# Two latent attentions: fp32 probabilities times values-and-ones in one plain product, in place of two-part products and a running sum

## The chip, the cores and the metric

The kernel runs on one core of a Trainium2 chip. The metric is the device time of one launch in microseconds (us), lower is better; a launch covers the whole network below. A core has five engines with instruction queues of their own: TensorE (PE; its weight loads are shown apart as PEld), VectorE (DVE), ScalarE (ACT), GpSimd (POOL) and SyncE (SP), which here issues every DMA.

## The reference

A two-layer network over 1024 latent tokens and 128 context tokens, 1024 channels, all in fp32. The mixers of the latent tokens are what matters here.

```python
# layer 0, multi-head latent attention: 8 heads, query/key width 96, value width 64, 1024 latent + 128 context keys
s = einsum('bqhd,bkhd->bhqk', q, k) * 96**-0.5
p = softmax(s, axis=-1)
out = einsum('bhqk,bkhd->bqhd', p, v)

# layer 1, neighbourhood attention: 16 heads of width 64, window of 8 x 16 grid positions, plus all 128 context keys
s_loc = einsum('bqhd,bikhd->bhqik', qr, kb) * 64**-0.5 + bias        # masked outside the window
s_ctx = einsum('bqhd,blhd->bhql', qr, k_ctx) * 64**-0.5
p = softmax(concat([s_loc, s_ctx]), axis=-1)
out = p_loc @ vb + p_ctx @ v_ctx
```

Around them: modulated norms, a combined input projection with a pooling mixer (layer 0), output projections, and a squared-relu MLP of width 4096 in each layer. The context tokens have small attentions of their own, which the change leaves as they are.

## The kernel before

**Number formats.** TensorE is fed in two ways. A tile of type F32R (shown as fp32r where DVE or ACT writes it) goes through as one product; where the accuracy of fp32 is wanted, an operand is split into two F32R tiles, high = rounded value, low = value minus high, and the products of the parts are added in PSUM (`mm3`). A product of two F32 tiles is a "plain" product.

**Stages.** Layer 0: input projection, norms, keys and queries; then the maxima of heads 0 and 1 woven with the values (`value_gen`), then the latent attention over heads 0 to 7 (`attend_units` woven with `max_units` of head h+2), then the output projection in two groups of tokens (`out_group`, helper `mm3`, lines L336 to L338, tile `ps_o`, residual at L891) while the rest of the modulation vectors is computed on DVE (`ada_gen`, L201, tile `trash`) and the attention's results are split (`split_groups`, L876 and L877, tile `oa`); then the MLP. Layer 1: projection, values (`value_gen1`), then the neighbourhood attention over heads 0 to 15 (`na_units` woven with `na_max` of head h+2, and for heads 0 to 6 with the context tokens' attention), then output projection and MLP. Loads of a head's operands are issued one or two heads ahead. What a scheduler makes of the program sets the order on each engine: it follows the written order of the units and may move independent instructions across each other.

**A unit of layer 0** is one head, 512 queries (a half), 128 keys. Scores come transposed, keys on partitions: three products into `ps_st` (L1079, L1082, L1083). ACT then takes the exponential twice from PSUM, once as F32R (`phi`, L1086) and once as F32 (`p`, L1087; for the first key tile straight into `ac`). DVE subtracts, `plo` = p - phi (L1088); POOL adds p to the running sum `ac` (L1090); and TensorE multiplies both parts with the values into `ps_pv` (L1091, L1092). 9 key tiles x 2 halves x 8 heads make 144 units. Each head's block of the stored values is 128 columns wide: 64 high parts and 64 low parts, so one product gives both; `split_values` (L998 on ACT, L999 on DVE) makes it, `vd0` and `vd` hold it in DRAM.

**The end of a half** (`finish_half`): ACT copies one half of the partitions of `ps_pv` (L1048), DVE adds it to the other (L1049); later, through the list `deferred`, a plain product of 64 columns of ones with `ac` (L1053, tile `ps_d`) sums the probabilities over the partitions, ACT copies that to `den` (L1054), and every second head `recip_pair` divides.

**A head of layer 1** takes the 128 context keys for each half (512 queries each; `ctx_unit`: exponentials into `chb` and `ac`, difference `clb`, L1326 to L1330, L1319) and 8 key tiles, of which two meet 256 queries and six 384, cut at the border of the halves (L1348 to L1357). Maxima (`na_max`) are 8 blocks of 512 columns, read by DVE (L1297).

**Buffers.** Large tiles share 36 slots, taken in the order in which they came free. A pair of units holds three slots before (`p`, `phi`, `plo`); `ac` takes a fourth in layer 0. PSUM tag "pa" (3 banks) serves `ps_st`, `ps_d`, `ps_o` and others, "pb" (3) the maxima, "pc" (2) `ps_pv`.

Of the kernel before, what the change touches and what calls it, by code (L numbers as in the profile page):

```python
# [10 lines left out]
F32 = mybir.dt.float32  # L11
# [79 lines left out]
def hybrid_kernel(ctx: ExitStack, tc: tile.TileContext, I, O):  # L91
# [255 lines left out]
    # Tokens go through in two groups of two halves of HC.  The first product takes hidden tiles j and j + NB, both  # L347
    # halves of the channels and both halves of the group as 2 x 2 blocks and forms the four results from seven products.
# [150 lines left out]
    # ================= layer 0 =================  # L499
# [29 lines left out]
    vd0 = DR("vd0", [9, P, D])  # L529

# [268 lines left out]
    vp = S.alloc("vp")  # L799

    def value_gen():
        for tt in range(10):
            ps = PS("ps_v")
            if tt < 9:
                ck = slice(tt * P, tt * P + P)
                nc.tensor.matmul(ps, ckv[0][:, ck], wk[1][:, 512:], start=True, stop=False)
                nc.tensor.matmul(ps, ckv[1][:, ck], wk[0][:, 512:], start=False, stop=False)
                nc.tensor.matmul(ps, ckv[0][:, ck], wk[0][:, 512:], start=False, stop=True)
            else:
                nc.tensor.matmul(ps, ckvc, wkf[:, 512:], start=True, stop=True)  # L810
            if tt == 8:
                nc.scalar.copy(vp[:, :512], ps)
            else:
                vs = S.alloc("vst", F32R)
                split_values(vs[:, :D], ps)
                dma(vd0[min(tt, 8)], vs[:, :D])
                S.free(vs)
            yield
        S.free(*ckv, small)
        S.free_ap(wkf)  # L820
# [160 lines left out]
    def load_rest(h):  # L981
        ql, kl, v = (S.alloc(n, F32R) for n in ("ql", "kl", "v"))
        n0, r0 = 64 * (h % 2), 32 * (h % 4)
        dma(ql[0:64, :NS], qd_n[1][h // 2, n0:n0 + 64, :])
        dma(ql[64:96, :NS], qd_r[1][h // 4, r0:r0 + 32, :])
        dma(kl[0:64, :], kd_n[1][h // 2, n0:n0 + 64, :])
        dma(kl[64:96, :], kd_r[1][h // 4, r0:r0 + 32, :])
        load_v(vd0, h, v)
        return ql, kl, v

    def load_v(vd, h, v):
        dma(v.rearrange("p (t f) -> p t f", t=9), vd[:, :, P * h:P * h + P].rearrange("t p f -> p t f"))
# [52 lines left out]
    def finish_half(par, half, po, ac, opair, den, last, store=None, ac_slot=True):  # L1045
        qs = slice(half * 512, half * 512 + 512)
        a = T("pva")
        nc.scalar.copy(a[par:par + 64], po[64 - par:128 - par])  # L1048
        nc.vector.tensor_add(opair[par:par + 64, qs], po[par:par + 64], a[par:par + 64])  # L1049

        def sums():
            pd = PS("ps_d")
            nc.tensor.matmul(pd[par:par + 64], ones[:, 0:64], ac[:, qs], start=True, stop=True)  # L1053
            nc.scalar.copy(den[par:par + 64, qs], pd[par:par + 64])  # L1054
            if half and ac_slot:
                S.free(ac)
            if last:
                recip_pair(opair, den)
                if store is not None:
                    dma(store, opair[:, :NS])  # L1060
                    S.free(opair)

        deferred.append(sums)

    def attend_units(h, qk, rest, opair, den):
        (qh, kh), (ql, kl, vv) = qk, rest
        v = vv.rearrange("p (t f) -> p t f", t=9)
        ac = S.alloc("ac")
        held = None
        for half in range(2):  # L1070
            qs = slice(half * 512, half * 512 + 512)
            po = PS("ps_pv", "pc")
            for kt in range(9):
                if held is None:
                    held, n = (S.alloc("p"), S.alloc("phi", F32R), S.alloc("plo", F32R)), 0
# [8 lines left out]
                p_ = ac[:, qs] if kt == 0 else held[0][:, u]  # L1084
                h_, l_ = held[1][:, u], held[2][:, u]
                nc.scalar.activation(h_, ps, AF.Exp, scale=scale0)  # L1086
                nc.scalar.activation(p_, ps, AF.Exp, scale=scale0)  # L1087
                nc.vector.tensor_sub(l_, p_, h_)  # L1088
                if kt:
                    nc.gpsimd.tensor_add(ac[:, qs], ac[:, qs], p_)  # L1090
                nc.tensor.matmul(po, v[:, kt, :], h_, start=kt == 0, stop=False)  # L1091
                nc.tensor.matmul(po, v[:, kt, :], l_, start=False, stop=kt == 8)  # L1092
                n += 1
                if n == 2:
                    S.free(*held)
                    held = None
# [3 lines left out]
            finish_half(64 * (h % 2), half, po, ac, opair, den, half and h % 2)  # L1100
# [46 lines left out]
    # ================= layer 1 =================  # L1147
# [29 lines left out]
    vd = DR("vd1", [9, P, 2 * D])  # L1177
# [21 lines left out]
    for i in range(2):  # L1199
        vs = S.alloc("vst", F32R)  # L1200
        split_values(vs[:, :D], vr[:, i * 512:i * 512 + 512])
        dma(vd[8][:, i * D:i * D + D], vs[:, :D])
        S.free(vs)
    S.free(vr)

# [62 lines left out]
    def load_na_rest(h):  # L1268
        k2, q2, v, tb = S.alloc("k2", F32R), W("wh", "q2"), S.alloc("nv", F32R), W("wr", "tb")
# [7 lines left out]
        load_v(vd, h, v)  # L1277
# [26 lines left out]
    def na_units(h, tl, rest, opair, den):  # L1304
# [3 lines left out]
        ac, chb, clb = W("wr", "ac"), W("wh", "chb"), W("wl", "clb")  # L1308
# [9 lines left out]
        def close_half(half):  # L1318
            nc.tensor.matmul(po[half], v3[:, 8, :], clb[:, half * 512:half * 512 + 512], start=False, stop=True)  # L1319
            finish_half(par, half, po[half], ac, opair, den, half and h % 2, od[h // 2][:, :NS] if h < 14 else None, False)  # L1320

        def ctx_unit(half):
# [3 lines left out]
            nc.scalar.activation(chb[:, qs], ps, AF.Exp)  # L1326
            nc.scalar.activation(ac[:, qs], ps, AF.Exp)
            nc.vector.tensor_sub(clb[:, qs], ac[:, qs], chb[:, qs])  # L1328
            po[half] = PS("ps_pv", "pc")
            nc.tensor.matmul(po[half], v3[:, 8, :], chb[:, qs], start=True, stop=False)  # L1330
# [4 lines left out]
        for i in range(8):  # L1335
# [3 lines left out]
            if held is None:  # L1339
                held, cnt = (S.alloc("p"), S.alloc("phi", F32R), S.alloc("plo", F32R)), 0  # L1340
            a, b = max(i - 1, 0) * P, min(i + 2, 8) * P
            n = b - a
            o = cnt * CH
            p_, hb, lb = (t[:, o:o + n] for t in held)
# [3 lines left out]
            nc.scalar.activation(hb, ps, AF.Exp)  # L1348
            nc.scalar.activation(p_, ps, AF.Exp)
            nc.vector.tensor_sub(lb, p_, hb)  # L1350
            nc.gpsimd.tensor_add(ac[:, a:b], ac[:, a:b], p_)  # L1351
            for half in range(2):
# [3 lines left out]
                for t in (hb, lb):  # L1356
                    nc.tensor.matmul(po[half][:, u - half * 512:w - half * 512], v3[:, i, :], t[:, u - a:w - a],  # L1357
                                     start=False, stop=False)
            cnt += 1
            if cnt == 3 or i == 7:  # L1360
                S.free(*held)
# [10 lines left out]
    def value_gen1():  # L1372
        for qt in range(4):
            ws = [wsplit(I["wv1"][qt, i]) for i in range(2)]
            fs = slice(qt * 256, qt * 256 + 256)
            for tt in range(9):
# [9 lines left out]
                else:  # L1386
                    if tt % 2 == 0:
                        vs = S.alloc("vst", F32R)
                    o = 512 * (tt % 2)
                    split_values(vs[:, o:o + 512], ps)  # L1390
                    if tt % 2:
                        dma(vd[tt - 1:tt + 1, :, qt * 512:qt * 512 + 512].rearrange("t p f -> p t f"),
                            vs[:, :D].rearrange("p (t f) -> p t f", t=2))
# [218 lines left out]
```

## Time and profile before

| | |
|---|---|
| timed runs | 3104.63 us median of 3 (3103.17 to 3110.44) |
| span of the profiled execution | 3107.1 us, mean granted TensorE clock 0.961 |
| its own time | the page gives the span alone; it lies between the timed runs |
| busy | PE 2968.8 us (96%), DVE 2427.3 (78%), ACT 1490.6 (48%), POOL 661.8 (21%) |
| layer 0 attention, first score product to last value product | 313.7 to 591.7 us |
| layer 0 output projection, up to the MLP's first product | 591.7 to 721.2 us |
| layer 1 attention, first context score product to last value product | 1890.1 to 2235 us |

Rows of groups read: line, engine, operation, names (out<-in), shapes, count | busy us, mean ns of one | idle time before them and what ended it. TensorE's records are pipelined: a product's recorded duration is longer than the distance to the next one's start. A plain product of the program stands as two records in the profile, so the 48 products of L1053 are 96 records. PEclk is the granted TensorE clock as a share of full speed. Window rows give, for each engine, its busy us and its instructions, then PEclk, the DMA engines' busy share and GB/s.

### The profile page before, as it was taken

The page shows a single profiled execution, that of the slowest core. Times are in us where ns is not written, and L with a number is a line of the kernel's source. Part 1 is how long each engine was busy: PE and PEld are TensorE (multiplying, and loading weights), DVE is VectorE, ACT ScalarE, POOL GpSimd, SP SyncE. Part 2 cuts the span into 40 slices and gives each one's busy share as a digit, 9 for nine tenths or more (in the row PEclk, how much of TensorE's full clock was granted, in tenths as well). Part 3 has the DMA queues.
Part 4 walks back from the last instruction along what each step waited for, and adds up shares of the span by engine and source line. Part 5 has one row for each costly group of instructions (what it writes and reads, how often), then busy time and mean ns, then how long its engine had stood idle before and what let it go on. Part 6 is the DMA issues. An engine that isn't in the chain of part 4 may idle for free.

```text
span 3107.1 us, 48559 instructions
## 1 busy us (share of the span) xinstructions
PE 2968.8 (96%) x18718; PEld 2673.4 (86%) x18718; DVE 2427.3 (78%) x4124; ACT 1490.6 (48%) x2546; POOL 661.8 (21%) x423
## 2 busy tenths in 40 slices
PE   7998998889999999999999999999999999999999
PEld 4956665689999999999988797666799999999999
DVE  5977999998668889786899534789777768877775
ACT  5364666434436534453645423667434445443433
POOL 1014777543000020000221002355421000010000
PEclk9996999899999999999999898899999999999999
DMA  6529222342223334232566345578302332332322
GB/s 229 165 71 319 63 60 48 121 136 84 90 85 92 103 129 143 89 96 87 169 206 199 108 178 151 151 186 227 127 28 76 95 95 79 114 93 87 102 75 85
DMA packets 148280, 376.03 MB, mean 121 GB/s; under 512 B 14225, under 2 KB 62977, under 8 KB 148050
## 3 DMA queue, kind: packets, MB, share of 16 engines
q1 hardware_dynamic: 148050, 372.94, 39.3%
q8 instruction: 147, 2.41, 0.3%
q14 instruction: 83, 0.68, 0.1%
HBM read 310.69 MB, written 61.01 MB: 120 GB/s over the span
## 4 chain that ended last, share of the span: by engine, by line
PE 67%; DVE 7%; DMA 3%; issue 2%; ACT 1%; POOL 1%; SPq 0%; DVEq 0%; POOLq 0%; ACTq 0%
PE ps L453 9%; PE ps L455 9%; PE ps L454 9%; PE ps L423 8%; PE ps L425 7%; PE ps L424 7%; PE ps_n L338 2%; PE ps_n L337 2%; PE ps_n L336 2%; PE ps_v L1381 1%; PE ps_v L1382 1%; PE ps_v L1383 1%; DVE trash L201 1%; DMA tb<-in_bias_k 1%; PE ps_o L336 1%
## 5 line engine op out<-in xcount | busy, mean ns | idle before, releaser
L453 PE MATMUL ps<-ml,wh 128*128 128x288 f32 x2048 | 591.9, 295 | 10.3 <-DVE ml L442 7.8
L454 PE MATMUL ps<-mh,wl 128*128 128x288 f32 x2048 | 600.8, 295 | 0.0
L455 PE MATMUL ps<-mh,wh 128*128 128x288 f32 x2048 | 596.5, 295 | 0.0
L423 PE MATMUL ps<-bl,wh 128*128 128x288 f32 x1792 | 532.7, 297 | 13.4 <-DVE bl L354 10.2
L424 PE MATMUL ps<-bh,wl 128*128 128x288 f32 x1792 | 529.5, 295 | 0.0
L425 PE MATMUL ps<-bh,wh 128*128 128x288 f32 x1792 | 527.9, 295 | 0.0
L453 PEld LDWEIGHTS ps<-ml,wh 128*128 128x128 f32 x2048 | 381.2, 188 | 11.3 <-DVE ml L442 8.3
L454 PEld LDWEIGHTS ps<-mh,wl 128*128 128x128 f32 x2048 | 385.2, 188 | 0.0
L455 PEld LDWEIGHTS ps<-mh,wh 128*128 128x128 f32 x2048 | 383.2, 188 | 0.1
L459 DVE SCALAR_TENSOR_TENSOR x<-ps,ada,x 128x288 f32<-128x288 f32 (+2 forms) x640 | 269.3, 450 | 113.2 <-PE ps L455 112.1
L423 PEld LDWEIGHTS ps<-bl,wh 128*128 128x128 f32 x1792 | 336.7, 188 | 16.7 <-issue 11.5
L425 PEld LDWEIGHTS ps<-bh,wh 128*128 128x128 f32 x1792 | 338.3, 189 | 0.0
L424 PEld LDWEIGHTS ps<-bh,wl 128*128 128x128 f32 x1792 | 337.3, 188 | 0.2
L396 ACT CAST wh<-s 128x512 fp32r<-128x512 f32 x256 | 146.1, 618 | 302.1 <-PE ps L455 216.1
L161 ACT CAST wh<-wr 128x1024 fp32r<-128x1024 f32 x188 | 196.9, 1049 | 177.3 <-PE ps L425 79.9
L162 POOL TENSOR_TENSOR wl<-wr,wh 128x1024 fp32r<-128x1024 f32 x44 | 119.6, 2723 | 731.4 <-ACT wh L161 722.8
L201 DVE CUSTOM_DVE_ANT_0 trash<-wada,silu 128x1024 bf16<-128x1024 f32 x160 | 216.1, 1351 | 17.9 <-DMA wada<-in_wada 6.2
L1351 POOL TENSOR_TENSOR ac<-ac,p 128x384 f32<-128x384 f32 (+1 forms) x128 | 151.8, 1186 | 367.2 <-DVE clb L1328 221.3
L1090 POOL TENSOR_TENSOR ac<-ac,p 128x512 f32<-128x512 f32 x128 | 202.9, 1587 | 67.1 <-ACT p L1087 35.0
L162 DVE TENSOR_TENSOR wl<-wr,wh 128x1024 fp32r<-128x1024 f32 x144 | 179.9, 1252 | 42.5 <-ACT wh L161 42.0
L396 ACT CAST wh<-wr 128x1024 fp32r<-128x1024 f32 (+1 forms) x128 | 106.9, 836 | 220.8 <-PE ps L455 150.7
L272 POOL TENSOR_TENSOR nt<-nt,sq 128x288 f32<-128x288 f32 (+1 forms) x45 | 50.7, 1129 | 706.8 <-ACT sq L271 697.5
(341 smaller groups left out, 7080.7 us busy)
## 6 DMA issues: line engine op xcount, KB each, us to landing
wr<-in_w SPq DMA_DIRECT2D x256, 512.0 KB
wada<-in_wada SPq DMA_DIRECT2D x48, 512.0 KB
wada<-in_wada0t SPq DMA_DIRECT2D x32, 512.0 KB
vd<-vst SPq DMA_DIRECT2D x27, 512.0 KB
wr<-in_win SPq DMA_DIRECT2D x24, 512.0 KB
wr<-in_wout SPq DMA_DIRECT2D x24, 512.0 KB
kk<-kd SPq DMA_DIRECT2D x32, 288.0 KB
nv<-vd SPq DMA_DIRECT2D x16, 576.0 KB
```

Of the source, the lines that this page charges most:

```text
L161: nc.scalar.copy(hi, r)
L162: (nc.gpsimd if e else nc.vector).tensor_sub(lo, r, hi)
L201: nc.vector.tensor_tensor_reduce(trash, r[:, :D], silu[i][:, :D], scale=1.0, scalar=0.0, op0=ALU.mult, op1=ALU.add, accum_out=a)
L396: nc.scalar.copy(h, src)
L423: nc.tensor.matmul(ps, wh[:, a], hl[:, b], start=k == 0, stop=False)
L424: nc.tensor.matmul(ps, wl[:, a], hh[:, b], start=False, stop=False)
L425: nc.tensor.matmul(ps, wh[:, a], hh[:, b], start=False, stop=k == 3)
L453: nc.tensor.matmul(ps, wh, hl, start=kk == 0, stop=False)
L454: nc.tensor.matmul(ps, wl, hh, start=False, stop=False)
L455: nc.tensor.matmul(ps, wh, hh, start=False, stop=kk == 3)
L459: nc.vector.scalar_tensor_tensor(x[m][:, a:b], ps[:, a - ch * HC:b - ch * HC], g, x[m][:, a:b], op0=ALU.mult, op1=ALU.add)
L1090: nc.gpsimd.tensor_add(ac[:, qs], ac[:, qs], p_)
```

## The change

Both attentions keep the probabilities whole, as F32, and the stored values as F32 in blocks of 192 columns for a pair of heads: values of the even head, 64 ones, values of the odd head. A head reads 128 of them (values and ones), so that one plain product per key tile gives the weighted values on 64 partitions and the sum of the probabilities on the other 64. Gone are the second exponential, the subtraction, POOL's running sum, the product with ones (L1053) and the addition at the end of a half; `finish_values` copies the values on DVE and the sums on ACT. `place_values` stores the values: a memset of ones on POOL and one copy on ACT.

```diff
     def load_rest(h):
-        ql, kl, v = (S.alloc(n, F32R) for n in ("ql", "kl", "v"))
+        ql, kl, v = S.alloc("ql", F32R), S.alloc("kl", F32R), S.alloc("v")
...
-    def split_values(o, src):
-        s4 = src.rearrange("p (g e f) -> p g e f", e=2, f=64)
-        o4 = o.rearrange("p (g e f) -> p g e f", e=4, f=64)
-        hi, lo = o4[:, :, 0:4:3], o4[:, :, 1:3]
-        nc.scalar.copy(hi, s4)
-        nc.vector.tensor_sub(lo, s4, hi)
+    def place_values(o, src):
+        o4 = o.rearrange("p (g e f) -> p g e f", e=3, f=64)
+        nc.gpsimd.memset(o4[:, :, 1], 1.0)
+        nc.scalar.copy(o4[:, :, 0:3:2], src.rearrange("p (g e f) -> p g e f", e=2, f=64))
+    def load_pv(vd, h, v):
+        o = 192 * (h // 2) + 64 * (h % 2)
+        dma(v.rearrange("p (t f) -> p t f", t=9), vd[:, :, o:o + P].rearrange("t p f -> p t f"))
+    def finish_values(par, half, po, opair, den, last, store=None):
+        qs = slice(half * 512, half * 512 + 512)
+        nc.vector.tensor_copy(opair[par:par + 64, qs], po[par:par + 64])
+        nc.scalar.copy(den[par:par + 64, qs], po[64 - par:128 - par])
+        def divide():
+            recip_pair(opair, den)
+            if store is not None:
+                dma(store, opair[:, :NS])
+                S.free(opair)
+        if last:
+            deferred.append(divide)
...
-    def finish_half(par, half, po, ac, opair, den, last, store=None, ac_slot=True):
...
     def attend_units(h, qk, rest, opair, den):
-        ac = S.alloc("ac")
-                    held, n = (S.alloc("p"), S.alloc("phi", F32R), S.alloc("plo", F32R)), 0
+                    held, n = S.alloc("p"), 0
-                p_ = ac[:, qs] if kt == 0 else held[0][:, u]
-                h_, l_ = held[1][:, u], held[2][:, u]
-                nc.scalar.activation(h_, ps, AF.Exp, scale=scale0)
+                p_ = held[:, u]
                 nc.scalar.activation(p_, ps, AF.Exp, scale=scale0)
-                nc.vector.tensor_sub(l_, p_, h_)
-                if kt:
-                    nc.gpsimd.tensor_add(ac[:, qs], ac[:, qs], p_)
-                nc.tensor.matmul(po, v[:, kt, :], h_, start=kt == 0, stop=False)
-                nc.tensor.matmul(po, v[:, kt, :], l_, start=False, stop=kt == 8)
+                nc.tensor.matmul(po, v[:, kt, :], p_, start=kt == 0, stop=kt == 8)
...
     def na_units(h, tl, rest, opair, den):
-        ac, chb, clb = W("wr", "ac"), W("wh", "chb"), W("wl", "clb")
+        cp = W("wr", "cp")
-            nc.scalar.activation(chb[:, qs], ps, AF.Exp)
-            nc.scalar.activation(ac[:, qs], ps, AF.Exp)
-            nc.vector.tensor_sub(clb[:, qs], ac[:, qs], chb[:, qs])
+            nc.scalar.activation(cp[:, qs], ps, AF.Exp)
-            nc.tensor.matmul(po[half], v3[:, 8, :], chb[:, qs], start=True, stop=False)
+            nc.tensor.matmul(po[half], v3[:, 8, :], cp[:, qs], start=True, stop=False)
-            nc.scalar.activation(hb, ps, AF.Exp)
             nc.scalar.activation(p_, ps, AF.Exp)
-            nc.vector.tensor_sub(lb, p_, hb)
-            nc.gpsimd.tensor_add(ac[:, a:b], ac[:, a:b], p_)
-                for t in (hb, lb):
-                    nc.tensor.matmul(po[half][:, u - half * 512:w - half * 512], v3[:, i, :], t[:, u - a:w - a],
-                                     start=False, stop=False)
+                nc.tensor.matmul(po[half][:, u - half * 512:w - half * 512], v3[:, i, :], p_[:, u - a:w - a],
+                                 start=False, stop=i == (4, 7)[half])
```

In layer 0's units TensorE's order before, for heads 0 to 5 (L1079, L1082, L1083 are the scores, L1091 and L1092 the value products, L1022 the maxima of a later head, L1053 the product with ones):

```order
L1079 MATMUL ps_st<-qh_2906,kl_3217 128x512
L1082 MATMUL ps_st<-ql_3216,kh_2907 128x512
L1083 MATMUL ps_st<-qh_2906,kh_2907 128x512
L1092 MATMUL ps_pv<-plo_3591,v_3218 128x512
L1091 MATMUL ps_pv<-phi_3590,v_3218 128x512
L1022 MATMUL ps_m<-kh_3546,qh_3545 128x384
L1053 MATMUL ps_d<-ac_3235,ones 64x512
L1092 MATMUL ps_pv<-plo_3591,v_3218 128x512
L1091 MATMUL ps_pv<-phi_3622,v_3218 128x512
```

And now at such a place (scores L1072, L1075, L1076, values L1079, maxima L1036):

```order
L1036 MATMUL ps_m<-kh_3258,qh_3257 128x384
L1072 MATMUL ps_st<-qh_2812,kl_3026 128x512
L1075 MATMUL ps_st<-ql_3025,kh_2813 128x512
L1076 MATMUL ps_st<-qh_2812,kh_2813 128x512
L1079 MATMUL ps_pv<-p_3313,v_3027 128x512
L1036 MATMUL ps_m<-kh_3258,qh_3257 128x384
```

Each unit has one value product where it had two, and it stands behind the scores of a later unit.

DVE's order before, at the last half of head 7 (L1088 is the subtraction, L1049 the addition, L876 and L877 the split for the output projection):

```order
L1049 TENSOR_TENSOR o_722_4491<-ps_pv,pva 64x512
L876 CAST oa_4973<-pooled_928 128x576
L1088 TENSOR_TENSOR plo_4875<-p_4873,phi_4874 128x512
L877 TENSOR_TENSOR oa_4973<-pooled_928,oa_4973 128x576
L876 CAST oa_4976<-pooled_928 128x576
L1088 TENSOR_TENSOR plo_4875<-p_4873,phi_4874 128x512
L1088 TENSOR_TENSOR plo_4898<-p_4896,phi_4897 128x512
L877 TENSOR_TENSOR oa_4976<-pooled_928,oa_4976 128x576
```

And now, from the first half of head 6 on (L1003 is the copy that ends a half; four of them belong to heads 6 and 7):

```order
L1003 COPY o_495_3912<-ps_pv 64x512
L876 CAST oa_4200<-pooled_928 128x576
L876 CAST oa_4197<-pooled_928 128x576
L877 TENSOR_TENSOR oa_4200<-pooled_928,oa_4200 128x576
L877 TENSOR_TENSOR oa_4197<-pooled_928,oa_4197 128x576
L1003 COPY o_495_3912<-ps_pv 64x512
L876 CAST oa_4203<-pooled_1031 128x576
```

The splits start two halves earlier; twelve of the sixteen, and the first of the modulation's products (L201), stand ahead of the last half's copy, where before the first split stood in the last half.

More of the change, by code (lines that the diff above doesn't have):

```diff
@@ L528, in hybrid_kernel @@
     kd_n, kd_r = [DR(f"kdn{i}", [4, P, TOK]) for i in range(2)], [DR(f"kdr{i}", [2, P, TOK]) for i in range(2)]
-    vd0 = DR("vd0", [9, P, D])
+    vd0 = DR("vd0", [9, P, 768], F32)
     hs = list(zip(hh, hl))
@@ L813, in value_gen @@
             else:
-                vs = S.alloc("vst", F32R)
-                split_values(vs[:, :D], ps)
-                dma(vd0[min(tt, 8)], vs[:, :D])
+                vs = S.alloc("vst")
+                place_values(vs[:, :768], ps)
+                dma(vd0[min(tt, 8)], vs[:, :768])
                 S.free(vs)
@@ L987, in load_rest @@
         dma(kl[64:96, :], kd_r[1][h // 4, r0:r0 + 32, :])
-        load_v(vd0, h, v)
+        load_pv(vd0, h, v)
         return ql, kl, v
-    def load_v(vd, h, v):
-        dma(v.rearrange("p (t f) -> p t f", t=9), vd[:, :, P * h:P * h + P].rearrange("t p f -> p t f"))
-    def split_values(o, src):
-        s4 = src.rearrange("p (g e f) -> p g e f", e=2, f=64)
-        o4 = o.rearrange("p (g e f) -> p g e f", e=4, f=64)
-        hi, lo = o4[:, :, 0:4:3], o4[:, :, 1:3]
-        nc.scalar.copy(hi, s4)
-        nc.vector.tensor_sub(lo, s4, hi)
+    def place_values(o, src):
[16 more added lines that the diff above has]
+            deferred.append(divide)
     def put_max(st, row, dst, d):
@@ L1043, in later @@
                 deferred.pop(0)()
-    def finish_half(par, half, po, ac, opair, den, last, store=None, ac_slot=True):
[L1046 to L1063, printed above, removed]
     def attend_units(h, qk, rest, opair, den):
@@ L1083, in attend_units @@
                 nc.tensor.matmul(ps, kh[0:97, ks], qh[0:97, qs], start=False, stop=True)
[L1084 to L1086 removed]
+                p_ = held[:, u]
                 nc.scalar.activation(p_, ps, AF.Exp, scale=scale0)
[L1088 to L1092 removed]
+                nc.tensor.matmul(po, v[:, kt, :], p_, start=kt == 0, stop=kt == 8)
                 n += 1
                 if n == 2:
[L1095 removed]
+                    S.free(held)
                     held = None
@@ L1099, in attend_units @@
                 yield
-            finish_half(64 * (h % 2), half, po, ac, opair, den, half and h % 2)
+            finish_values(64 * (h % 2), half, po, opair, den, half and h % 2)
         yield
@@ L1176, in hybrid_kernel @@
     kd = [DR(f"kd1{i}", [8, P, TOK]) for i in range(2)]
-    vd = DR("vd1", [9, P, 2 * D])
+    vd = DR("vd1", [9, P, 1536], F32)
     nc.vector.tensor_scalar_mul(V("naq"), V("naq"), NA_SCALE)
@@ L1199, in hybrid_kernel @@
     for i in range(2):
-        vs = S.alloc("vst", F32R)
-        split_values(vs[:, :D], vr[:, i * 512:i * 512 + 512])
-        dma(vd[8][:, i * D:i * D + D], vs[:, :D])
+        vs = S.alloc("vst")
+        place_values(vs[:, :768], vr[:, i * 512:i * 512 + 512])
+        dma(vd[8][:, i * 768:i * 768 + 768], vs[:, :768])
         S.free(vs)
@@ L1268, in load_na_rest @@
     def load_na_rest(h):
-        k2, q2, v, tb = S.alloc("k2", F32R), W("wh", "q2"), S.alloc("nv", F32R), W("wr", "tb")
+        k2, q2, v, tb = S.alloc("k2", F32R), W("wh", "q2"), S.alloc("nv"), W("wr", "tb")
         p, n0 = h // 2, 64 * (h % 2)
@@ L1276, in load_na_rest @@
         dma(tb[:, :640], I["bias_k"][h])
-        load_v(vd, h, v)
+        load_pv(vd, h, v)
         th, tl = W("wl", "tbh"), S.alloc("tbl", F32R)
@@ L1318, in close_half @@
         def close_half(half):
-            nc.tensor.matmul(po[half], v3[:, 8, :], clb[:, half * 512:half * 512 + 512], start=False, stop=True)
-            finish_half(par, half, po[half], ac, opair, den, half and h % 2, od[h // 2][:, :NS] if h < 14 else None, False)
+            finish_values(par, half, po[half], opair, den, half and h % 2, od[h // 2][:, :NS] if h < 14 else None)
         def ctx_unit(half):
@@ L1339, in na_units @@
             if held is None:
-                held, cnt = (S.alloc("p"), S.alloc("phi", F32R), S.alloc("plo", F32R)), 0
+                held, cnt = S.alloc("p"), 0
             a, b = max(i - 1, 0) * P, min(i + 2, 8) * P
             n = b - a
-            o = cnt * CH
-            p_, hb, lb = (t[:, o:o + n] for t in held)
+            p_ = held[:, cnt * CH:cnt * CH + n]
             ps = PS("ps_st")[:, :n]
@@ L1355, in na_units @@
                     continue
-                for t in (hb, lb):
-                    nc.tensor.matmul(po[half][:, u - half * 512:w - half * 512], v3[:, i, :], t[:, u - a:w - a],
-                                     start=False, stop=False)
+                nc.tensor.matmul(po[half][:, u - half * 512:w - half * 512], v3[:, i, :], p_[:, u - a:w - a],
+                                 start=False, stop=i == (4, 7)[half])
             cnt += 1
             if cnt == 3 or i == 7:
-                S.free(*held)
+                S.free(held)
                 held = None
@@ L1387, in value_gen1 @@
                     if tt % 2 == 0:
-                        vs = S.alloc("vst", F32R)
-                    o = 512 * (tt % 2)
-                    split_values(vs[:, o:o + 512], ps)
+                        vs = S.alloc("vst")
+                    o = 384 * (tt % 2)
+                    place_values(vs[:, o:o + 384], ps)
                     if tt % 2:
-                        dma(vd[tt - 1:tt + 1, :, qt * 512:qt * 512 + 512].rearrange("t p f -> p t f"),
-                            vs[:, :D].rearrange("p (t f) -> p t f", t=2))
+                        dma(vd[tt - 1:tt + 1, :, qt * 384:qt * 384 + 384].rearrange("t p f -> p t f"),
+                            vs[:, :768].rearrange("p (t f) -> p t f", t=2))
                         S.free(vs)
```

## Prediction

> **What bounds the kernel now.** I read the page first, then busy time by stretch, then the groups and waits of the two attentions.
>
> ```profile
> span 3107.1 us, 48559 instructions
> PE 2968.8 (96%) x18718; PEld 2673.4 (86%) x18718; DVE 2427.3 (78%) x4124; ACT 1490.6 (48%) x2546; POOL 661.8 (21%) x423
> PE   7998998889999999999999999999999999999999
> DVE  5977999998668889786899534789777768877775
> PEclk9996999899999999999999898899999999999999
> ```
>
> PE looks like the bound everywhere, but its records overlap and stretch when it waits. The stretches show another picture (the attention of layer 0, the output projection behind it, the attention of layer 1 in all, its heads 0 to 6, its heads 7 to 14):
>
> ```profile
> core 0: us, PE busy (x) PEld busy (x) DVE busy (x) ACT busy (x) POOL busy (x), PEclk, DMA share, GB/s
> 313.70:591.70 278.00, 246.24 (x899) 166.74 (x898) 264.78 (x320) 178.94 (x334) 210.77 (x131) 0.92 0.25 67
> 591.70:721.20 129.50, 110.84 (x764) 109.33 (x763) 125.23 (x173) 40.06 (x64) 57.68 (x23) 0.91 0.38 121
> 1890.10:2235.00 344.90, 322.42 (x1507) 235.06 (x1505) 279.07 (x517) 209.38 (x475) 169.06 (x135) 0.89 0.65 174
> 1890.10:2056.70 166.60, 154.03 (x683) 109.17 (x681) 116.47 (x253) 95.53 (x233) 66.53 (x59) 0.83 0.64 164
> 2056.70:2197.00 140.30, 135.06 (x657) 97.10 (x658) 129.32 (x225) 98.46 (x214) 83.23 (x67) 0.95 0.73 199
> ```
>
> In the first two DVE is busy for 95% and 97%, in heads 7 to 14 of layer 1 for 92%, and the clock is below 1, so PE idles. What DVE and POOL do in the first:
>
> ```profile
> L1088 DVE TENSOR_TENSOR plo<-p,phi 128x512 fp32r<-128x512 f32 x128 | 154.5, 1225 | 4.6 <-ACT p L1087 4.4
> L1023 DVE TENSOR_REDUCE stat<-ps_m 128x1 f32<-128x384 f32 x129 | 66.9, 545 | 8.5 <-PE ps_m L1022 8.3
> L1088 DVE TENSOR_TENSOR plo<-ac,phi 128x512 fp32r<-128x512 f32 x16 | 18.8, 1178 | 0.0
> L1090 POOL TENSOR_TENSOR ac<-ac,p 128x512 f32<-128x512 f32 x128 | 202.9, 1587 | 67.1 <-ACT p L1087 35.0 <-issue 11.4 <-DVE plo L1088 5.3
> PEld ps_pv L1092 <- DVE plo L1088: 53.6, 62, 3.6
> ```
>
> The subtractions are 173 of DVE's 265 us, and the value product of the low part is what waits for them. I take DVE as the bound of layer 0's attention, with PE next. PE's own price is the distance between starts:
>
> ```profile
> 423.00 0.40 PE L1092 MATMUL ps_pv<-plo,v 128*128 128x512 f32 x1
> 423.24 0.40 PE L1091 MATMUL ps_pv<-phi,v 128*128 128x512 f32 x1
> 423.47 0.34 PE L1022 MATMUL ps_m<-kh,qh 96*128 96x384 f32 x1
> 423.74 1.07 PE L1053 MATMUL ps_d<-ac,ones 128*64 128x512 f32 x2
> 424.75 0.50 PE L1092 MATMUL ps_pv<-plo,v 128*128 128x512 f32 x1
> ...
> 111.10 0.81 PE L606 MATMUL ps_l<-sql,ones 128*128 128x384 f32 x2
> 111.45 0.63 PE L338 MATMUL ps_i<-hh,wh 128*128 128x384 f32 x1
> 111.92 0.34 PE L336 MATMUL ps_i<-hl,wh 128*128 128x384 f32 x1
> 112.09 0.34 PE L337 MATMUL ps_i<-hh,wl 128*128 128x384 f32 x1
> ```
>
> A split product of 512 columns takes 0.23 us (423.24 to 423.47), 0.45 ns a column; of 384, 0.17 us. The plain product with 64 ones took 1.01 us. The plain one with all 128 columns of weights (L606) went from 111.10 to 111.92 together with one product of 0.17 behind it: 0.65 us for 384 columns, 1.69 ns a column, 0.87 us for 512. The new value product has 128 columns of weights, so I take 0.87; 1.01 is the upper end.
>
> **The change, part by part.** Layer 0's attention. PE now: 144 units of five products, 144 x 5 x 0.23 = 166; 129 maxima x 0.17 = 22; 16 products with ones x 1.01 = 16; together 204 of 278 us. Then: 144 x 3 x 0.23 = 99, 22, and 144 x 0.87 = 125: 246 us. PE gets 42 us more, and DVE loses 173 and keeps about 91, ACT loses one of two exponentials (row below, 87 us), POOL nearly all.
>
> ```profile
> L1086 ACT ACTIVATE phi<-ps_st 128x512 fp32r<-128x512 f32 x144 | 86.8, 602 | 70.4 <-PE ps_st L1083 54.2 <-POOL ac L1090 5.3 <-DVE den L1034 3.9
> L1053 PE MATMUL ps_d<-ac,ones 128*64 128x512 f32 x96 | 62.6, 739 | 0.1
> ```
>
> So the bound moves to PE. A unit's exponential (0.60) has a whole unit of PE (1.56 with its product) to hide in, because the value product stands behind a later unit's scores. Beside the 246 I leave 14 us for the start, for seven changes of head and for part of a slow clock: 260, a gain of 18. Ends: 32 (nothing beside the 246) and 0.
>
> The output projection behind it. PE's steps there do not change. DVE's splits go into the attention, where DVE now has room, and the modulation's products begin earlier. PE's waits in that stretch:
>
> ```profile
> PE ps_n L275 <- DVE nt L273: 9.8, 2, 7.5
> PE ps_o L336 <- DVE oa L877: 5.1, 1, 5.1
> PE ps_o L336 <- DVE x L891: 3.8, 1, 3.8
> ```
>
> The 5.1 should go, most of the 9.8 too; with the clock back I take 12 us. What is late next is x (3.8), as now. Ends: 0 (another DVE instruction stands there) and 25 (all three waits, 18.7, and half of the clock's 0.09 x 129.5 = 12).
>
> Layer 1's attention. In a head of columns: scores, bias and maxima are 2 x 1024 + 4 x 2816 + 4096 = 17,408 columns (2816 = 2 x 256 + 6 x 384), 7.8 us at 0.45 ns; values 2 x 3840, 3.5 us; two products with ones, 2.0 us: 13.3 us. Then 3840 plain columns, 6.5 us, and no ones: 14.3 us, 1.0 more. Heads 7 to 14 take 140.3 / 8 = 17.5 us, heads 0 to 6 take 23.8. DVE's rows there:
>
> ```profile
> L1350 DVE TENSOR_TENSOR plo<-p,phi 128x384 fp32r<-128x384 f32 x96 | 88.8, 938 | 9.0 <-ACT p L1349 8.8
> L1328 DVE TENSOR_TENSOR clb<-ac,chb 128x512 fp32r<-128x512 f32 x32 | 21.9, 685 | 15.9 <-ACT ac L1327 15.9
> L1350 DVE TENSOR_TENSOR plo<-p,phi 128x256 fp32r<-128x256 f32 x32 | 18.7, 585 | 1.1 <-ACT p L1349 1.0
> ```
>
> 129 of DVE's 279 us go. Heads 7 to 14 come to PE's 14.3 and 2 us of waits, 16.3: 10 us gained. Heads 0 to 6 also carry the context tokens' attention and a start that waits for loads; I put them at 20 us: 7 x 3.8 = 27 gained. The last head, where DVE and POOL finish sums, 5. Together 42; ends 15 (heads 0 to 6 stay load-bound) and 75 (all heads at 16).
>
> The smaller parts. Storing the values loses a DVE subtraction and gains a POOL memset; both run beside PE's long products, 3 us at most in layer 0's preparation, where DVE was busy. Loads have the same count and size. The end of a half: the DVE addition becomes a copy and ACT makes one copy instead of two; neither is on PE's path with two banks for `ps_pv`. Fewer slots per pair give loads more room; I cost this inside the 42. Other stages are unchanged; another choice of slots may move them by 5 us either way.
>
> Sum: 18 + 12 + 42 + 3 = 75 off the span of 3107.1, 3032. The span lies 2.5 us above the median of the timed runs, so 3030. A measurement of this kernel tells no change from one under about 0.3%, 9 us.
>
> A rule on the clock weighs here. The rows: the granted clock was 0.92, 0.91 and 0.89 where PE waits. The Trainium skill ("TensorE: Matmul & The Clock Gate", Part 1) says that the clock falls to half after an idle window of about 3.4 us and comes back after as long a busy one. By that rule a PE-bound attention would run at full clock, and layer 0's would lose nothing but its start, 250 us; with a clock that stays at its row it would take 246 / 0.92 = 267 before any wait. My 260 lies between the two.
>
> **The rivals.** *The clock and the waits stay.* The maxima's banks and late loads still interrupt PE. For it: PE waits for DVE's maxima and for loads today. Against it: DVE and ACT lose a third or more. Then layer 0 takes 267 + 9 = 276, a gain of 2, the projection 5, layer 1 about 20: 3078.
>
> *Layer 1 stays bound by loads.* For it: SP, one queue in order, waits in heads 0 to 6 for what the maxima send:
>
> ```profile
> SPq L113 <- ACT row L1010: 26.3, 5, 17.4
> SPq L113 <- PE ps_st L1316: 23.1, 8, 6.9
> SPq L113 <- DMA mrow<-row: 16.4, 6, 6.8
> ```
>
> Against it: heads 7 to 14 get loads at 199 GB/s against 164 and need 17.5 us. If the heads keep their times but for 8 us, the gain is 18 + 12 + 3 + 8 = 41: 3064.
>
> *Slower: the plain product costs more than its row.* The two attentions hold 144 + 16 x 7.5 = 264 plain products of 512 columns. Each 0.1 us more costs 26 us, so at 0.87 + 75 / 264 = 1.15 us nothing is left. The records of L1053 cover 62.6 us for 48 products, 1.30 each; at that price the sum is 3030 + 264 x 0.43 = 3144. Against it: that figure holds stretches at half clock and narrow weights, and 1.01 itself would leave 3030 + 37 = 3067.
>
> *The product isn't plain.* Were F32 operands taken in one pass, PE would gain 264 x 0.64 = 169 us more, 2860. Against it: each plain product here has two records.
>
> **How the numbers follow.** All three stretches shorten, 40 to 120 us gained: 0.70. Clock and waits stay: 0.11. Loads bind layer 1: 0.12. Slower: 0.04. Not plain: 0.01. Nothing measurable, as parts cancel: 0.02. The likeliest is 3030. The range takes the likeliest case's ends short of their joint extremes and the two smaller gains: 2985 to 3080. Faster 0.93, same 0.03, slower 0.04.
>
> **What would show it.** Starts of neighbouring value products and scores in layer 0: 0.87 us between a value product and the next instruction, two records each. DVE's share of layer 0's attention near a third, PE's clock there above 0.97, and the stretch 255 to 265 us. The output projection at 115 to 120 us with no wait for `oa`. Heads 7 to 14 of layer 1 at about 16 us, heads 0 to 6 at about 20. Wrong would be: PE still waiting for DVE's maxima in layer 0, SP's waits unchanged in layer 1, or a plain step above 1 us.

## The result and the profile after

The changed kernel takes 3058.22 us (median of 4, 3052.10 to 3061.23), the kernel before on the same chip 3103.90 (3098.63 to 3110.44): a ratio of 0.9845, 95% interval 0.9813 to 0.9878. That is 46 us faster by the medians and 48 by the ratio, where 75 were forecast (3030, range 2985 to 3080). The page of the profile after:

```profile
span 3057.2 us, 46985 instructions
PE 2950.9 (97%) x18622; PEld 2663.1 (87%) x18622; DVE 2117.4 (69%) x3777; ACT 1337.7 (44%) x2194; POOL 315.5 (10%) x210
PE   7998999889999999999999999989989999999999
DVE  5976343797768889786899522544677678777775
PEclk9996999999999999999999999999999999999999
```

DVE lost 310 busy us, POOL 346, ACT 153, and the span lost 49.9. By stretch (layer 0's attention, the projection behind it, layer 1's attention, its heads 0 to 6, its heads 7 to 14):

```profile
314.20:568.60 254.40, 254.40 (x887) 164.84 (x886) 99.70 (x184) 101.49 (x172) 7.14 (x3) 0.99 0.26 70
568.60:699.00 130.40, 106.94 (x746) 105.62 (x745) 120.81 (x165) 41.07 (x65) 57.75 (x23) 0.90 0.36 113
1864.50:2185.70 321.20, 303.57 (x1442) 228.88 (x1441) 160.18 (x358) 133.55 (x284) 16.57 (x7) 0.95 0.71 188
1864.50:2011.50 147.00, 140.86 (x663) 102.08 (x662) 73.10 (x191) 62.50 (x150) 7.11 (x3) 0.92 0.69 178
2011.50:2154.50 143.00, 132.47 (x618) 99.52 (x619) 68.20 (x144) 59.71 (x118) 9.46 (x4) 0.96 0.76 200
```

Layer 0's attention went from 278.0 to 254.4, layer 1's from 344.9 to 321.2, and the projection in between from 129.5 to 130.4. The stretch of layer 1 ahead of its attention, where the values are stored, went from 381.8 to 375.9. The rest moved by 2.5 or less.

In layer 0 the groups of rows show the new balance, and the starts of neighbouring products the price of a plain one:

```profile
L1079 PE MATMUL ps_pv<-p,v 128*128 128x512 f32 x288 | 147.2, 593 | 0.0
L1078 ACT ACTIVATE p<-ps_st 128x512 f32<-128x512 f32 x144 | 85.9, 596 | 141.6 <-PE ps_st L1076 141.5
L1037 DVE TENSOR_REDUCE stat<-ps_m 128x1 f32<-128x384 f32 x129 | 67.6, 553 | 102.3 <-PE ps_m L1036 102.1
...
422.87 1.02 PE L1079 MATMUL ps_pv<-p,v 128*128 128x512 f32 x2
423.32 0.74 PE L1036 MATMUL ps_m<-kh,qh 96*128 96x384 f32 x1
423.90 0.39 PE L1072 MATMUL ps_st<-qh,kl 96*128 96x512 f32 x1
```

ACT and DVE both stand waiting for TensorE, for 142 and 102 us. From 422.87 to 423.90 passes 1.03 us for one value product (two records) and one maxima product of 0.17: 0.86 for the plain product, against 0.87 taken from the row of L606.

The projection's waits of TensorE, and what the engines did between the end of the last half and the last split:

```profile
PE ps_o L336 <- DVE oa L877: 10.9, 1, 10.9
PE ps_n L275 <- DVE nt L273: 8.9, 1, 8.9
PE ps_o L336 <- DVE x L891: 3.7, 2, 3.2
```

```profile
569.83 0.70 DVE L1003 COPY o<-ps_pv 64x512 f32<-64x512 f32 x1
...
573.68 3.21 DVE L201 CUSTOM_DVE_ANT_0 trash<-wada,silu 128x1024 bf16<-128x1024 f32 x1 [0.85 <-DMA wada<-in_wada0t]
576.93 3.29 DVE L201 CUSTOM_DVE_ANT_0 trash<-wada,silu 128x1024 bf16<-128x1024 f32 x1
580.26 1.23 DVE L201 CUSTOM_DVE_ANT_0 trash<-wada,silu 128x1024 bf16<-128x1024 f32 x1
581.41 1.22 DVE L1048 SCALAR_TENSOR_TENSOR den<-den,ry 128x1024 f32<-128x1024 f32 x1
582.55 1.22 DVE L201 CUSTOM_DVE_ANT_0 trash<-wada,silu 128x1024 bf16<-128x1024 f32 x1
583.69 1.22 DVE L1049 SCALAR_TENSOR_TENSOR o<-o,den 128x1024 f32<-128x1024 f32 x1
...
573.41 2.40 POOL L1047 TENSOR_TENSOR den<-den,ry 128x1024 f32<-128x1024 f32 x1 [56.24 <-ACT ry L1046]
575.89 3.24 POOL L162 TENSOR_TENSOR wl<-wr,wh 128x1024 fp32r<-128x1024 f32 x1
```

POOL's step of the last division was ready at 575.81; DVE's step of it (L1048) began at 581.41, because three modulation products (L201) stand ahead of it in DVE's queue (two of them drawn out beside POOL, see the last section), and a fourth stands ahead of L1049. The split that TensorE needs comes after those. The wait for `oa`, which the prediction struck out, doubled from 5.1 to 10.9.

In layer 1's attention SyncE's waits for the rows of maxima and for their store, before and then after:

```profile
SPq L113 <- ACT row L1010: 30.9, 8, 17.4
SPq L113 <- DMA mrow<-row: 38.8, 13, 7.1
...
SPq L113 <- ACT row L1024: 36.9, 11, 7.8
SPq L113 <- DMA mrow<-row: 38.5, 14, 8.0
```

The change did not shorten them.

### The profile page after: what moved, and what is told of

Read it like the earlier page. It is cut to its first block, busy times and chain, and to the rows that moved or that the text cites. A ratio compares the mean times of both kernels' runs of the same rounds, so it can differ in the third digit from the quotient of the medians.

```text
span 3057.2 us, 46985 instructions
## 1 busy us (share of the span) xinstructions
PE 2950.9 (97%) x18622; PEld 2663.1 (87%) x18622; DVE 2117.4 (69%) x3777; ACT 1337.7 (44%) x2194; POOL 315.5 (10%) x210
## 4 chain that ended last, share of the span: by engine, by line
PE 86%; DVE 5%; DMA 5%; issue 1%; ACT 1%; POOL 1%; SPq 0%; DVEq 0%; ACTq 0%; POOLq 0%
PE ps L453 9%; PE ps L455 9%; PE ps L454 9%; PE ps L423 8%; PE ps L425 7%; PE ps L424 7%; PE ps_pv L1079 4%; PE ps_pv L1336 2%; PE ps_n L336 2%; PE ps_n L337 2%; PE ps_n L338 2%; PE ps_v L1360 1%; DVE trash L201 1%; PE ps_v L1362 1%; PE ps_v L1361 1%
## 5 line engine op out<-in xcount | busy, mean ns | idle before, releaser
L423 PEld LDWEIGHTS ps<-bl,wh 128*128 128x128 f32 x1792 | 336.7, 188 | 16.5 <-issue 11.5
L201 DVE CUSTOM_DVE_ANT_0 trash<-wada,silu 128x1024 bf16<-128x1024 f32 x160 | 214.5, 1340 | 17.9 <-DMA wada<-in_wada 7.6
L1037 DVE TENSOR_REDUCE stat<-ps_m 128x1 f32<-128x384 f32 x192 | 98.3, 551 | 121.2 <-PE ps_m L1036 120.9
L1284 DVE CUSTOM_DVE_ANT_0 trash<-ps_m,ta 128x512 bf16<-128x512 f32 (+1 forms) x128 | 84.0, 656 | 122.0 <-PE ps_m L1282 113.4
L397 DVE TENSOR_TENSOR wl<-s,wh 128x512 fp32r<-128x512 f32 x232 | 157.6, 711 | 5.1 <-ACT wh L396 2.8
```

What stands on the lines that cost most here:

```text
L201: nc.vector.tensor_tensor_reduce(trash, r[:, :D], silu[i][:, :D], scale=1.0, scalar=0.0, op0=ALU.mult, op1=ALU.add, accum_out=a)
L397: (nc.gpsimd if j in EDGE and min(ps) in EDGE_POOL else nc.vector).tensor_sub(l, src, h)
L423: nc.tensor.matmul(ps, wh[:, a], hl[:, b], start=k == 0, stop=False)
```

## The experiments

Each was timed beside the kernel before on one chip; ratios are to that. "Layer 0's attention" and the other stretches are cut at the same instructions as above; heads 7 to 14 run from head 7's first exponential of context scores to head 15's.

**Layer 0 alone.** The kernel before with the new `load_rest`, `attend_units`, `place_values` and `value_gen`; layer 1 keeps `finish_half`, split probabilities and the running sum.

> The kernel before with layer 0's attention alone in the new form; layer 1 as before. If the stages gain separately: layer 0's attention 254 us (278 before), the projection behind it 130 as in both kernels, layer 1's attention 345, and the whole 3104 - 24 = 3080. The rival, that slots and late loads couple the layers, puts layer 1's attention under 335 and the whole at 3070 or less, or loses part of layer 0's 24 again.

Measured: 3081.52 us, ratio 0.9918 (0.9897 to 0.9938).

```profile
311.70:563.40 251.70, 251.70 (x887) 162.87 (x886) 99.92 (x184) 101.48 (x172) 7.13 (x3) 1.00 0.26 70
1861.20:2214.60 353.40, 328.68 (x1507) 240.04 (x1506) 277.71 (x517) 210.16 (x475) 173.04 (x135) 0.87 0.64 170
```

Layer 0's attention gains 26 and the whole 25: the layers gain separately, and about half of the change's 48 is layer 0's. Layer 1's attention is in its old form here and took 353.4. In the three other profiles with that form it took 344.9, 338.2 and 338.6. The four span 15 us, so a difference of that size between single profiles of layer 1's attention shows nothing by itself.

**One pass.** The changed kernel with `p`, `cp` and the values as F32R:

```diff
-                    held, n = S.alloc("p"), 0
+                    held, n = S.alloc("p", F32R), 0
-    vd0 = DR("vd0", [9, P, 768], F32)
+    vd0 = DR("vd0", [9, P, 768])
-        cp = W("wr", "cp")
+        cp = W("wh", "cp")
```

and so on for `v`, `nv`, `vst` and layer 1.

> The changed kernel with probabilities and stored values as F32R, so that the value product goes in one pass; the low parts are left out. Each of the 264 products of 512 columns costs 0.64 us less. My theory: layer 0's attention is bound by TensorE and falls by 144 x 0.64 = 92 us, from 254 to about 162; layer 1's heads 7 to 14 are held by loads and stay at 16 to 18 us, so the whole is about 2945. The rival, TensorE binds layer 1 too: heads 7 to 14 come down by 4.8 us each to 13, and the whole is about 2895. A second rival, layer 0 is held by the maxima or the exponentials: its attention stays above 200.

Measured: 2936.57 us, ratio 0.9449 (0.9427 to 0.9471). Layer 0's attention, then heads 7 to 14 of layer 1:

```profile
312.10:474.80 162.70, 162.70 (x749) 136.47 (x748) 97.72 (x183) 100.64 (x172) 7.19 (x3) 1.00 0.41 108
1899.80:2036.10 136.30, 109.78 (x541) 90.49 (x540) 71.16 (x157) 59.83 (x119) 9.93 (x4) 0.81 0.85 231
```

Layer 0 falls by 91.7 of the 92 expected: with the change, TensorE alone binds it. Heads 7 to 14 take 17.0 us each against 17.9, although TensorE lost 4.8 of its 14.3: something that the value product does not touch binds these heads. The DMA queues are busy for 85% and move 231 GB/s. How much is gained depends on the cut. At the start of head 15 TensorE has begun its scores and waits for the row of maxima:

```profile
PE ps_st L1303 <- DMA q<-mrow: 6.7, 2, 4.9
```

Cut at the first score products of heads 7 and 15, the heads take 129.7 us here, 16.2 each, and still 17.9 in the changed kernel. So TensorE's 4.8 us bring 0.9 to 1.7 a head.

**The bias table first.** In layer 1 ACT stands before the cast of the bias table `tb`, which is loaded behind the row of maxima. The experiment issues that load first.

```diff
+        dma(tb[:, :640], I["bias_k"][h])
         dma(k2[0:64], kd[0][p, rows])
...
-        dma(tb[:, :640], I["bias_k"][h])
```

> The changed kernel with one line moved: the load of a head's bias table (tb) is issued first of the head's second set of loads, ahead of the row of maxima, for which SyncE waits. My theory: ScalarE stands for 34 us in layer 1 before the cast of tb, with the exponentials behind it; these 34 go to under 10, layer 1's attention comes from 321 to about 300, the whole to about 3037. The rival, that the row of maxima or the slots hold the heads anyway: layer 1's attention stays above 316, the whole at 3053 to 3060.

Measured: 3054.02 us, ratio 0.9829 (0.9808 to 0.9850), no difference from the changed kernel. The wait before and now:

```profile
ACT tbh L1266 <- DMA tb<-in_bias_k: 33.9, 10, 6.9
...
ACT tbh L1266 <- DMA tb<-in_bias_k: 40.1, 11, 8.0
```

My theory fell: the load is issued earlier and lands no earlier against its need. ACT's wait is where the lateness shows, and not its cause.

**Fewer bytes.** Two of a head's loads bring rows that another tile already holds; POOL, which is idle for nine tenths of that time, copies them instead.

```diff
-        dma(qq[64:128, :NS], qd[0][p, rows])
+        nc.gpsimd.tensor_copy(qq[64:128, :NS], qq[0:64, :NS])
-        dma(k2[0:64], kd[0][p, rows])
+        nc.gpsimd.tensor_copy(k2[0:64], kk[0:64])
```

> The changed kernel with two of layer 1's loads replaced by copies on GpSimd from the tile that already holds the same rows: the second half of qq and the keys of k2; 544 of about 3570 KB a head are no longer loaded. My theory: the bytes of the loads bind heads 7 to 14 (28.5 MB at 200 GB/s with the DMA queues busy for 76%); they come from 17.9 to 15.5 to 16.5 us, the heads 0 to 6 from 20.9 to 19 to 20, layer 1's attention from 321 to 295 to 305, the whole to about 3038. The rival: SyncE's order and the row of maxima bind, not the bytes; layer 1's attention stays above 316 and the whole at 3053 to 3060. Second rival: the copies stand behind the division on GpSimd and hold the next head, slower than 3060.

Measured: 3035.97 us, ratio 0.9768 (0.9742 to 0.9794), 22 us below the changed kernel. All of layer 1's attention, heads 0 to 6, heads 7 to 14:

```profile
1859.10:2162.20 303.10, 295.07 (x1442) 223.06 (x1441) 161.97 (x358) 133.76 (x284) 45.56 (x34) 0.98 0.64 174
1859.10:1996.20 137.10, 134.34 (x664) 96.89 (x663) 74.09 (x194) 62.45 (x149) 24.20 (x19) 0.98 0.64 161
1996.20:2129.70 133.50, 130.32 (x616) 98.77 (x616) 68.78 (x141) 59.93 (x117) 21.36 (x15) 0.97 0.66 186
```

321.2 became 303.1 (301.6 in the run with both edits, below); heads 7 to 14 take 16.7, a little above the 15.5 to 16.5 expected, heads 0 to 6 19.6 us. In heads 7 to 14 the queues moved 24.87 MB instead of 28.54, 13% less. Fewer loads shorten the attention though the order of those that are left is the same, so the order alone is not what held it. The edit takes away issues as well as bytes, though: in the same heads SyncE issues 78 DMAs in 33.4 us where it issued 89 in 43.1, while its waits stay (102 us in all, 99 after the change). Which of the two shortens the heads, the bytes or the issues, this run can't tell.

**Modulation products earlier.** The 32 late products (L201) and their loads written between the units of heads 2 to 7 of layer 0:

```diff
+    late = ada_late()
     for h in range(8):
...
+        if h > 1:
+            gs.append((islice(late, 6), 6))
         weave(*gs)
...
-    run(ada_late())
+    run(late)
```

> The changed kernel with the 32 late modulation products of layer 0 (L201) and their loads written between the units of heads 2 to 7 of the attention instead of behind it. My theory: the projection is held by VectorE, where these products take 53 of 130 us and stand ahead of the last division; it falls to about 108, the attention grows by at most 4 for its share of VectorE, and the whole is about 3040. First rival: the products stand ahead of the maxima and the attention loses what the projection gains, 3055 to 3060. Second rival: the projection is held by its weights (loads and their splits on GpSimd) and stays above 122.

Measured: 3034.08 us, ratio 0.9763 (0.9738 to 0.9789). Attention and projection of layer 0:

```profile
312.70:572.50 259.80, 257.13 (x890) 164.75 (x889) 135.87 (x252) 101.45 (x172) 7.17 (x3) 0.99 0.35 98
572.50:676.80 104.30, 100.53 (x742) 99.85 (x741) 69.59 (x93) 41.99 (x65) 48.69 (x23) 0.98 0.22 66
```

The projection falls from 130.4 to 104.3, the attention pays 5.4. The profiled execution (span 3021.8) was one of the shorter ones, with 310.6 us for layer 1's attention; the medians differ by 24, about what layer 0 shows.

**The same move in the kernel before.** The edit above, applied to the kernel before.

> The kernel before with the modulation products written between the units of heads 2 to 7. My theory: VectorE has only 13 idle us of 278 there, so the 53 us of these products lengthen the attention by 35 to 45, the projection falls by about 25, and the whole is 3110 to 3125; the room for this move is made by the change. The rival: the move is good by itself, whatever the value product, and gives 3075 to 3090.

Measured: 3123.28 us, ratio 1.0053 (1.0029 to 1.0077): slower.

```profile
313.30:633.10 319.80, 267.45 (x899) 179.22 (x898) 305.89 (x389) 179.37 (x334) 222.54 (x131) 0.86 0.30 85
633.10:740.40 107.30, 103.78 (x763) 103.10 (x763) 75.20 (x103) 40.36 (x64) 51.56 (x23) 0.98 0.21 65
```

The projection falls to 107.3 here too, and the attention takes 41.8 us more, with DVE busy for 306 of 320. The time that the change frees on DVE is what pays for the move.

**The order alone.** Two lines exchanged, so that the last splits are written ahead of the modulation products:

```diff
-    run(ada_late())
     acts += [split_groups(o) for o in opairs]
+    run(ada_late())
```

> The changed kernel with two lines of the program exchanged: the splits of the last attention results are written ahead of the late modulation products, so that VectorE divides and splits heads 6 and 7 before any of these products. My theory: the projection is held by VectorE's total (120 of 130 us), and the order alone gains nothing: TensorE's wait for oa goes from 10.9 to under 5, waits for the second norm grow instead, the projection stays at 126 to 134 and the whole at 3053 to 3064. The rival: the products ahead of the last division are the cause, and the projection falls to 116 to 121, the whole to 3044 to 3049.

Measured: 3052.41 us, ratio 0.9819 (0.9790 to 0.9847). The wait and the stretch:

```profile
PE ps_o L336 <- DVE oa L877: 2.4, 1, 2.4
...
569.30:685.10 115.80, 99.32 (x695) 97.82 (x694) 109.25 (x150) 40.44 (x63) 50.61 (x21) 0.93 0.40 132
```

The stretch shrinks to 115.8, as the rival said, but part of that is only a first MLP product that starts earlier, among the projection's last ones. From the end of the attention to the end of the MLP it is 912.9 us against 920.0 after the change, 893.9 with the products moved into the attention, and 916.6 before. In the four runs above that change the kernel elsewhere (layer 0 alone, one pass, the bias table first, fewer bytes) this length is 920.1 to 920.7. So the order is worth about 7 us of the 26. Most of the rest is taken to be DVE's load in that stretch, since TensorE's waits there name DVE alone, but the move takes the loads of these products away too. By the medians, whose intervals overlap, the 7 us can be seen only in the trace.

**No running sum.** The kernel before without POOL's additions in layer 0 (L1090), so that its sums of probabilities hold the first key tile alone, with a constant 1 added where they are copied:

```diff
-            nc.scalar.copy(den[par:par + 64, qs], pd[par:par + 64])
+            nc.scalar.activation(den[par:par + 64, qs], pd[par:par + 64], AF.Copy, bias=1.0)
...
-                if kt:
-                    nc.gpsimd.tensor_add(ac[:, qs], ac[:, qs], p_)
```

> The kernel before with GpSimd's additions to the running sum of layer 0 (L1090) left out, so its sums of probabilities hold the first key tile alone (and a constant of 1 against zeros); everything else is as before. My theory: GpSimd's additions slow VectorE's subtractions (1225 ns mean, 671 the shortest); without them the subtractions come to 0.67 to 0.75 us, VectorE to about 190 us, and layer 0's attention falls from 278 to 215 to 230, bound by TensorE's 204; the whole about 3050. The rival: the subtractions cost 1.2 us by themselves, VectorE stays the bound, and the attention stays above 265.

Measured: 3052.52 us, ratio 0.9832 (0.9799 to 0.9864).

```profile
313.90:538.60 224.70, 220.03 (x915) 166.27 (x914) 183.26 (x321) 178.44 (x335) 8.41 (x4) 0.98 0.30 81
L1088 DVE TENSOR_TENSOR plo<-p,phi 128x512 fp32r<-128x512 f32 x128 | 88.5, 698 | 22.3 <-ACT p L1087 21.5 <-DMA x<-in_xT 0.5
```

The same subtraction takes 698 ns instead of 1225, DVE 183 us instead of 265, and layer 0's attention 224.7 instead of 278.0. So about 82 of the 265 us that count as DVE's work there, a third, were waiting for POOL; in the subtractions it is 72 of 173. Of the things that the change removes, this one addition is worth 53 us in that stretch; the whole change gives 23.6, since its plain products put 42 us onto TensorE.

**Copies and earlier products together.**

> The changed kernel with the modulation products written between the units of heads 2 to 7 (as in the run before) and the copies on GpSimd in place of two loads. If the two gains are of different stages they add: 3034 - 20 = about 3014. The rival, that the earlier products have already taken the load-bound part of layer 1 (311 us there against 321): about 3026.

Measured: 3014.63 us, ratio 0.9701 (0.9674 to 0.9727), 44 us below the changed kernel. The gains add; this is the fastest version here that keeps the arithmetic of the change.

**Both, in one pass.**

> The one-pass kernel (probabilities and values as F32R, low parts left out) with both other edits, the earlier modulation products and the copies in place of two loads. TensorE needs 9.4 us a head of layer 1 there, so what is left is the loads. My theory: heads 7 to 14 go with the bytes, 17.0 x 3030 / 3570 = 14.4 us, layer 1's attention from 293 to about 265; layer 0's attention takes the products beside 163 us and comes to 165 to 178, the projection to 104; the whole 2885 to 2900. The rival: an order of waits, not the bytes, holds the heads; they stay at 16.3 or more, and the whole at 2910 to 2920.

Measured: 2912.35 us, ratio 0.9377 (0.9344 to 0.9410). Layer 0's attention, layer 1's, and its heads 7 to 14:

```profile
312.20:507.00 194.80, 181.98 (x749) 145.03 (x748) 135.05 (x252) 101.31 (x172) 8.02 (x3) 0.92 0.45 132
1778.30:2038.00 259.70, 245.58 (x1249) 202.81 (x1248) 160.78 (x358) 132.03 (x283) 45.43 (x33) 0.88 0.71 199
1901.90:2011.80 109.90, 104.47 (x526) 88.11 (x526) 64.08 (x142) 58.77 (x116) 21.64 (x15) 0.86 0.83 235
```

Layer 1 came out as the bytes said: 13.7 us a head for 14.4 expected, 259.7 for 265. SyncE's issues over these heads fell by about as large a share as the bytes, from 94 in the one-pass run to 78, so here too bytes and issues can't be told apart. Layer 0 was missed: 194.8 for 165 to 178. That puts the whole into the rival's range (2910 to 2920), though the heads went as the theory said. DVE is busy for only 135 us in layer 0's attention; TensorE's weight loads and its products wait for DVE's maxima:

```profile
PEld ps_m L1036 <- DVE stat L1037: 10.1, 14, 2.0
PE ps_m L1036 <- DVE stat L1037: 5.1, 9, 1.6
```

In the one-pass run without the move the weight loads waited 0.3 us for them. Modulation products of 1.2 us that stand ahead of the maxima would do this. How much of the 32 us it is, no run here tells.

## Why the prediction was right and wrong

- **The whole (75 forecast, 46 measured): right in direction and inside the range, 28 us from the likeliest.** It lies nearer to the rival "Layer 1 stays bound by loads" (3064). That nearness is partly luck: the rival took 18, 12 and 3 for the other parts and 8 for layer 1's attention, where 23.6, nothing, nothing that can be seen and 24 came.
- **Layer 0's attention (18 forecast, 23.6 measured): right.** The plain product costs 0.86 us, TensorE's sum of 246 lies under a stretch of 254.4 at a granted clock of 0.99, and the one-pass run takes off 91.7 of 92. The steady clock of the rows would have had 267. The rule of the Trainium skill that the prediction cites ("TensorE: Matmul & The Clock Gate", Part 1) would have had 250; the 254.4 lie nearer to that. The reading of the stretch before as bound by DVE was right too, though what DVE's 173 us of subtractions were made of was missed: 72 of them were waiting for POOL's additions.
- **The projection (12 forecast, nothing gained): wrong.** The failed step is "The 5.1 should go". The splits did move into the attention, twelve of sixteen. But the two of heads 6 and 7 hang on the last division, and TensorE waits for one of them. When POOL's step of that division is done, four modulation products still stand ahead of and between DVE's two steps. They were counted as work that begins earlier, and not as work that stands ahead of something; only the lower end, 0, allowed for it. The larger miss is the stage's total: DVE had 125 of 129.5 us of work there and still has 120.8, and only 4 of it left. Moving the products and their loads away gave 26, their order alone about 7.
- **Layer 1's attention (42 forecast, 24 measured): half wrong.** The 24 hold beyond single profiles: the four of the old form have a mean of 343.8 us, the four with the changed layer 1 (the changed kernel, the bias table first, the modulation products earlier, the order alone) 319.7. Heads 0 to 6 gained 19.6 us where 27 were forecast (23.8 to 21.0 a head, for 20), the last head 7 for 5. The failed term is "Heads 7 to 14 come to PE's 14.3 and 2 us of waits, 16.3": they took 17.9, no less than the 17.5 before, at 200 GB/s as before. (Cut at the score products, the same eight profiles have 17.3 to 18.3 with the change and 17.4 to 18.1 without.) The rival that loads bind was right for these heads. Whether it was right for its reason, SyncE's order of waits, is open. The prediction's sign of being wrong, SyncE's waits unchanged in layer 1, came true for the rows of maxima (75.4 us, 69.7 before); but with fewer loads heads 7 to 14 got shorter while SyncE's waits over them stayed at about 100 us in all (for the rows of maxima they fell from 39.9 to 26.5). The 199 GB/s beside 164 were taken as a sign that loads had room.
- **What holds heads 7 to 14: open in part.** The most that any run moved over such heads is 231 and 235 GB/s; by an estimate from these, at 233 the 28.5 MB need 122 of the 143 us, more than TensorE's 8 x 14.3 = 114. Issuing the table's load earlier gave nothing; 13% fewer bytes in 12% fewer issues gave 1.2 us a head, TensorE's 4.8 us less gave 0.9 (1.7 by the other cut), and both together 4.2. So these heads are held by loads and TensorE together, with the loads probably the nearer of the two, and neither hides under the other as the 2 us of waits assumed. Whether a load costs by its bytes, its issue or its place in SyncE's order, and which waits tie loads and TensorE together, is not settled by these runs.
- **The smaller parts (3 forecast in layer 0): not to be seen.** Layer 0's preparation did not change. The stretch of layer 1 that stores the values took 376 to 382 us in four profiles with the old form (mean 378.6) and 372 to 379 in eight with the new (375.3); the 5.9 between the two pages is partly that spread.
- **The slower rivals** had no part: the plain product's price is that of its row.

## What to carry to other kernels

When an engine is taken off the path, price what is left in each stage by itself: the queue of an engine that stays full, and the loads that a head needs whatever its arithmetic. A stretch that keeps its length and its GB/s when the engines in it lose half of their work points to its loads; a wait for a load that does not shorten when the load is issued earlier says the same. And before an engine is relieved of work, ask whether the work is slow or waits for a neighbour: here one addition on POOL took the subtractions on DVE from 698 to 1225 ns, and a kernel without it gained 53 us in that stage, where the whole change gained 23.6. That kernel lacks the sums, so this is the price of the addition and not yet a version to use.

## What the hardware showed

In these traces a DVE instruction with two operands in SBUF stands still while POOL works on SBUF. In the rows above, L201 takes 1.23 us alone (580.26) and 3.21 and 3.29 us beside POOL: POOL's instruction ends at 573.41 + 2.40 = 575.81 and the product at 576.89, 1.08 later; the next POOL instruction ends at 579.13 and the next product at 580.22, 1.09 later. Nearly the whole product runs after POOL has ended. POOL appears to wait in its turn: its second instruction (575.89) takes 3.24 us, where the same one, starting ahead of DVE's, takes 2.40 later on, and DVE's product beside it is the long one again:

```profile
594.11 2.40 POOL L162 TENSOR_TENSOR wl<-wr,wh 128x1024 fp32r<-128x1024 f32 x1 [14.97 <-ACT wh L161]
...
594.34 3.25 DVE L201 CUSTOM_DVE_ANT_0 trash<-wada,silu 128x1024 bf16<-128x1024 f32 x1
```

The Trainium skill ("SBUF — State Buffer", SBUF: two separate sides) has this as a lock: DVE and GpSimd share a pair of ports, and the one that comes first holds it for its whole instruction. The trace agrees, and so do the subtractions at 1225 and 698 ns with and without POOL's additions.
